# Seven products of block sums in place of eight for three quarters of an up projection, in a two-layer decoder step on one core

## The chip, the core and the metric

The kernel is one program on one core of a Trainium2 chip. Its time is the device time of one execution in microseconds (us). TensorE (PE) does the matmuls; VectorE (DVE), ScalarE (ACT) and GpSimd (POOL) do everything else; SyncE (SP) only issues transfers.

## The reference

Two layers of a decoder work on 576 tokens: one prompt of 512, and 8 samples of 8 new tokens. Each layer mixes tokens in three branches and then runs an MLP. What matters here, for the tokens x of one layer:

```python
rq, rk, rv, rg, sq, sk, sv, mq, g_ret, g_swa, g_mem = split(x @ w_in)
# retention, sliding-window attention, attention into 256 memory tokens
merged = sigmoid(g_ret) * ret_b + sigmoid(g_swa) * swa_b + sigmoid(g_mem) * mem_b
x = layer_norm(ALPHA * x + merged @ w_out, ln1_g, ln1_b)
h = jnp.square(jax.nn.relu(x @ w_up))             # (576, 1024) @ (1024, 4096)
return layer_norm(ALPHA * x + h @ w_down, ln2_g, ln2_b)   # (576, 4096) @ (4096, 1024)
```

The prompt attends to 256 memory tokens that the layer computes; each sample attends to memory keys and values of its own, which come from caches (`in_mck`, `in_mcv`).

## The kernel before

Activations are kept with features on the 128 partitions and tokens along the columns, in two token groups: A has 256 columns, B 320 (`NG`, `OFF`). All weights are laid out beforehand as 154 units per layer, each a tile of 128 x 8 x 128 f32 (512 KB), in the order in which they are used (`unit_order`); SP fetches them in that order from `in_wall`. An output tile of 128 features for one group is the sum of 8 slots of a unit over 1,024 inputs.

Matmuls run in fp32r. To keep the accuracy of f32, each operand is split into a rounded part and the rest, and each slot takes three matmuls: hi by xh, lo by xh, hi by xl (`gemm`). So one unit is 24 matmuls for group A (`pg<-A,...`) and 24 for B (`mstep`, `both`).

`split` prepares a unit. For `up` and `dn` units, ACT casts the raw tile to hi (CAST 128x1024), writes the negative of hi to lo (ACTIVATE 128x1024), and POOL issues a transfer that adds the raw tile to lo (accumulate DMA, `A<-A` or `B<-A` on POOL). So lo is there when that transfer has landed. The other units get lo by a subtraction on DVE or POOL. Tiles come from two pools of 25 (tag A) and 15 (tag B) buffers; a tile that finds none free waits for the last reader of the oldest.

The MLP stage goes through four chunks of the 4,096 hidden features: 8 `up` units, then 8 `dn` units. An `up` output is evacuated by ACT as relu, square, cast (`up_ev`), and a subtraction for its low part; a `dn` output is added by DVE onto `y` in SBUF.

The order of instructions on every engine is fixed while the program is built. `run` walks over the products; after every six matmuls `Filler.advance` emits other work that is due by a model of the engines (`Clock`), and `tick` emits the next unit's split when its use, as planned by `plan` with `mm_us` per matmul, is within `LOOK`, when no more than `cap` units are split and unused, and when ACT is free or the use is nearer than `LEAD` = 4 us. An engine then executes its rows strictly in that order. The program's instructions are all recorded by one helper (L331 before, L358 after), so that the names of tiles tell them apart.

In the sample part of the memory attention (`mem_sample`), scores `pa` of four samples are taken one after the other, 8 short matmuls each; two key tiles are loaded ahead by POOL, the others in turn as earlier samples' matmuls are emitted. The value tiles follow in the same way.

Of the kernel before, what the change touches and what calls it, by code (L numbers as in the profile page):

```python
# [21 lines left out]
NB = 8  # L22
# [4 lines left out]
NG = {"A": 256, "B": 320}  # L27
OFF = {"A": 0, "B": 256}
TOK = SEQ + NB * NT
UNITS = 154  # L30
SKEW_WO = 8
# [11 lines left out]
N_A = 25  # L43
N_B = 15
# [18 lines left out]
def unit_order():  # L63
    o = [("mk", m) for m in range(4)] + [("mv", i) for i in range(4)]
    for p in range(4):
        o += [("rk", p), ("rq", p), ("rv", p, 0), ("rv", p, 1), ("rg", 2 * p), ("rg", 2 * p + 1)]
    o += [("sv", 0), ("sk", 0)] + [("sq", m) for m in range(4)]
    for m in range(8):
        o += [("gr", m), ("br", m)]
    o += [("mq", m) for m in range(4)]  # L70
    for g, b in (("gs", "bs"), ("gm", "bm")):
        for i in range(4):
            o += [(g, 2 * i), (g, 2 * i + 1), (b, i)]
    o += [("wo", m) for m in range(8)]
    for c in range(4):
        o += [("up", c, m) for m in range(8)] + [("dn", c, m) for m in range(8)]
    return o


def pack_weights(w_in, w_br_ret, w_br_swa, w_br_mem, w_out, w_mem_kv, w_up, w_down):  # L80
# [13 lines left out]
    for l in range(DEPTH):  # L94
        wb_swa = w_br_swa[l][swa_rows]
        for u, key in enumerate(order):
# [29 lines left out]
            elif k == "up":  # L126
                v = full(w_up[l], (m * 8 + key[2]) * P + np.arange(P))
            else:
                v = full(w_down[l][m * 1024:(m + 1) * 1024], key[2] * P + np.arange(P))
# [4 lines left out]
def make_consts():  # L134
# [4 lines left out]
    pos = np.concatenate([np.arange(SEQ), np.tile(PAST + np.arange(NT), NB)]).astype(np.float32)  # L139
# [59 lines left out]
def mm_us(n):  # L199
    return n / 2400.0 + 0.0025  # L200


def plan():
    a, b = 24 * mm_us(256), 24 * mm_us(320)
    t, out = 0.0, []
    order = unit_order()
    for l in range(DEPTH):
        i = 0
        while i < UNITS:
            k = order[i][0]  # L210
            if k in ("mk", "mv"):
                out.append(t)
                t += a
            elif l and order[i] == ("rk", 0):
                out += [t, t + a]
                t += 2 * (a + b)
                i += 1
            elif k == "rv":
                out += [t, t]
                t += 4.67 * a  # L220
                i += 1
            elif order[i] in (("wo", 8 - SKEW_WO), ("up", 0, 0), ("dn", 3, 8 - dn_skew(l))):
                s = {"dn": dn_skew(l), "wo": SKEW_WO, "up": SKEW_UP}[k]
                for j in range(s):
                    out.append(t)
                    t += a if k != "dn" or l < DEPTH - 1 else b
                t += s * (b if k != "dn" or l < DEPTH - 1 else a)
                i += s - 1
            else:
                out.append(t)  # L230
                t += a + b
            i += 1
# [117 lines left out]
class Filler:  # L350
# [48 lines left out]

    def finish(self, gen):  # L400
# [15 lines left out]
class Builder:  # L416
    def __init__(self, nc, tc, I, O, coff, pools):
# [9 lines left out]
        self.done = -1  # L427
        self.cap = 4
        self.use = plan()
# [3 lines left out]
    def tile(self, shape, dt=F32, tag="A", bufs=None):  # L433
        self.n += 1
        bufs = bufs or {"A": N_A, "B": N_B}[tag]
# [16 lines left out]
    def u(self, n=320):  # L452
        return self.tile([P, 320], tag="u", bufs=5)[:, :n]

    def tt(self):
        return self.tile([P, 320], tag="t", bufs=4)
# [52 lines left out]
    def fetch(self, u):  # L509
        self.raw[u] = self.tile([P, 8, P], tag="A")  # L510
# [4 lines left out]
    def split(self, u):  # L515
        raw = self.raw.pop(u)
        k = unit_order()[u % UNITS]
        if k[0] == "wo":
            b = True
        elif k[0] in ("up", "dn"):  # L520
            b = u % 2 == 0
        else:
            b = k[0] in ("gr", "br") and u % 4 == 0
        tl = "B" if b else "A"
        hi = self.tile([P, 8, P], F32R)
        lo = self.tile([P, 8, P], F32R, tag=tl)
        if k[0] in ("up", "dn"):
# [5 lines left out]
        self.w[u] = (hi, lo)  # L533

    def tick(self):
        n, u = len(self.use), self.split_next
# [3 lines left out]
        urgent = self.use[u] < self.fill.t + LEAD  # L540
# [3 lines left out]
    def feed(self):  # L544
        while self.dma_next <= min(self.split_next + 2, len(self.use) - 1):
# [5 lines left out]
    def run(self, steps, cap=3):  # L551
# [5 lines left out]
        for i, (units, fn, tick) in enumerate(steps):  # L557
# [3 lines left out]
            for u in units:  # L561
                if last[u] == i:
                    self.done = max(self.done, u)
# [4 lines left out]
    def gemm(self, ps, u, slots, xs):  # L568
# [4 lines left out]
        for i, s in enumerate(slots):  # L573
            xh, xl = xs(i)
            mm(ps, lhsT=hi[:, s, :], rhs=xh, start=(i == 0), stop=False)
            mm(ps, lhsT=lo[:, s, :], rhs=xh, start=False, stop=False)
            mm(ps, lhsT=hi[:, s, :], rhs=xl, start=False, stop=(i == n - 1))
# [14 lines left out]

    def pair_tiles(self, dt=F32):
        return {"A": self.tile([P, 4, 256], dt, tag="A"), "B": self.tile([P, 4, 320], dt, tag="B")}

    def feat_tiles(self, nt):
        r = {}
        for g in "AB":
            r[g] = {"h": [], "l": []}
            for k in "hl":  # L600
                for j in range(nt):
                    r[g][k].append(self.tile([P, 4, NG[g]], F32R, tag=g))
        return r

    def load_x(self, X):
# [5 lines left out]
        def part(g, j):  # L611
            raw = self.tile([P, 4, NG[g]], tag=g)
# [9 lines left out]
        def split():  # L622
            for i in range(4):
# [5 lines left out]
                h = self.tile([P, 4, NG[g]], F32R, tag=g)  # L629
                lo = self.tile([P, 4, NG[g]], F32R, tag=g)  # L630
# [70 lines left out]
    def norm_ev(self, g, y, l, gi, eps, out, scale=None, bias=1.0):  # L701
# [33 lines left out]
        def half():  # L735
            c = st.pop("c")
            V.tensor_tensor(y[0], y[0], c.unsqueeze(1).to_broadcast([P, 4, n]), ALU.subtract)
            sq = self.tile([P, 4, n], tag=g)
# [7 lines left out]
        def last():  # L746
# [4 lines left out]
            t = self.tile([P, 320], tag="ln", bufs=2)[:, :n]  # L751
# [8 lines left out]
            r0 = self.tile([P, 320], tag="ln", bufs=2)[:, :n]  # L760
# [7 lines left out]
            a = self.tile([P, 320], tag="ln", bufs=2)[:, :n]  # L768
# [27 lines left out]
            if out is not None:  # L796
                out[g]["h"] += [self.tile([P, 4, n], F32R, tag=g) for _ in range(2)]
                out[g]["l"] += [self.tile([P, 4, n], F32R, tag=g) for _ in range(2)]
# [64 lines left out]

    def rope_evac(self, ps, out, o, n):
# [7 lines left out]
    def retention(self, l, p, qk, rv, sg, GR):  # L872
# [11 lines left out]
        yield Pe((qk, rv))  # L884
        v2 = self.tile([P, 2, 256], F32R)
        self.split_into(v2[:64, 0], v2[:64, 1], rv[:64, 4, :])
# [9 lines left out]
        for e in range(2):  # L896
            r = slice(e * 64, e * 64 + 64)
            for c in range(4):
                cs = slice(c * P, (c + 1) * P)
                T.matmul(pq[e][:, cs], lhsT=k[r, cs], rhs=q[r, cs], start=True, stop=True)  # L900
# [8 lines left out]
        for c in range(4):  # L909
            cs = slice(c * P, (c + 1) * P)  # L910
            T.transpose(pk[:, cs], k[:, cs], ident)
        px = [self.bank("a"), self.bank("a")]
        for e in range(2):
            r = slice(e * 64, e * 64 + 64)
            T.matmul(px[e][:64, P:P + 64], lhsT=k[r, 512:576], rhs=q[r, 512:576], start=True, stop=True)
        T.transpose(px[0][:64, 0:P], k[:, 512:576], ident)
# [17 lines left out]
        V.tensor_tensor(kq[:, 1].rearrange("p (c i) -> p c i", c=4), q[:, 0:512].rearrange("p (c i) -> p c i", c=4),  # L934
# [8 lines left out]
        for f in range(2):  # L943
            for e in range(2):
                r = slice(e * 64, e * 64 + 64)
                dst = self.qz[f * 64:f * 64 + 64, e, f * 32:f * 32 + 288].rearrange("p (b c) -> p b c", b=4)[:, :, 0:8]
                V.tensor_tensor(dst, q[r, 512 + f * 32:544 + f * 32].rearrange("p (b t) -> p b t", b=4),
# [11 lines left out]
        for bb in range(5):  # L959
            for e in range(2):  # L960
# [4 lines left out]
                else:  # L965
                    T.matmul(o, lhsT=ks[:, 256 + e * 64:320 + e * 64], rhs=rv[:64, 4, e * P:(e + 1) * P],
# [34 lines left out]
        gs = self.tile([P, P], tag="u", bufs=5)  # L1001
# [11 lines left out]
        wt = self.tile([P, 2, 512])  # L1013
        ws = self.tile([P, 2, 64], tag="ws", bufs=1)
# [8 lines left out]
        for e in range(2):  # L1023
            yield (ps[e],)
            V.scalar_tensor_tensor(wt[:, e], ps[e], gg[:, e:e + 1], sg[:, e, 0:512], ALU.mult, ALU.mult)
            V.scalar_tensor_tensor(ws[:, e], pt[:, e * 64:e * 64 + 64], gg[:, e:e + 1], sg[:, e, 512:576],
                                   ALU.mult, ALU.mult)
        yield (wt, ws)
        for src, g_, a, b in ((wt[:, :, 0:256], "A", 0, 256), (wt[:, :, 256:512], "B", 0, 256), (ws, "B", 256, 320)):
# [748 lines left out]
```

## Time and profile before

| | |
|---|---|
| time, median of 3 runs | 2186.92 us (2186.02 to 2187.66) |
| profiled execution | 2185.91 us, span 2184.1 us |
| granted TensorE clock, mean | 0.997 of full speed |
| busy in the span | PE 2147.9 us (98%), DVE 1060.2 (49%), ACT 846.9 (39%), POOL 411.2 (19%) |
| DMA | 130 GB/s mean |

The span runs from the first to the last instruction of the profiled execution; 1.8 us of that execution's time lie outside it. PE works in nearly all of it, so what bounds the kernel is looked for in PE's rows and its waits.

### The profile page before, as it was taken

Reading aid. Unit: us, or ns where it says so; the run is one execution under the profiler, and the core shown is the slowest. Engines: PE = TensorE matmul, PEld = TensorE weight load, DVE = VectorE, ACT = ScalarE, POOL = GpSimd, SP = SyncE. Lnnn points to the kernel's source line nnn. Section 1 sums busy time; section 2 is a strip of 40 time slices with the busy share of each in tenths; the row PEclk is TensorE's granted clock in tenths of the full one; section 3 lists DMA queues with packets and bytes.
Section 4 is the critical chain, followed back from the end, with each engine's and each line's share of the span. In section 5 each row is a group of like instructions: output and inputs, shape, how many; then the busy total and the mean of one; then the engine's idle time right before and its main releaser. Section 6 shows DMA issues by size and latency. Waiting matters only on the chain. (4 is left out here: it accounts for less than half of the span.)

```text
span 2184.1 us, 39229 instructions
## 1 busy us (share of the span) xinstructions
PE 2147.9 (98%) x16466; PEld 2089.6 (96%) x16466; DVE 1060.2 (49%) x2164; ACT 846.9 (39%) x1581; POOL 411.2 (19%) x400
## 2 busy tenths in 40 slices
PE   9999999999999999999999999999999999999996
PEld 9999999999999999999989998999999999999996
DVE  6666765455566111111876668554555751111127
ACT  3222234232146454636342221442221573636362
POOL 0222300011033111111432223000210321111113
PEclk9999999999999999999999999999999999999999
DMA  8222212334255867676452222123443557676661
GB/s 308 78 90 86 91 49 69 116 135 137 98 169 126 201 143 185 153 195 161 125 178 84 84 84 83 59 68 107 145 153 124 144 126 195 148 187 159 174 150 45
DMA packets 85168, 284.56 MB, mean 130 GB/s; under 512 B 9280, under 2 KB 19008, under 8 KB 84928
## 3 DMA queue, kind: packets, MB, share of 16 engines
q1 hardware_dynamic: 50944, 168.27, 22.2%
q0 software_dynamic: 28960, 105.92, 22.0%
q10 hardware_dynamic: 5088, 7.87, 1.1%
q8 instruction: 129, 2.11, 0.4%
q14 instruction: 47, 0.39, 0.1%
HBM read 200.89 MB, written 15.99 MB: 99 GB/s over the span
## 5 line engine op out<-in xcount | busy, mean ns | idle before, releaser
L331 PE MATMUL pg<-B,A 128*128 128x320 f32 x5920 | 1024.7, 310 | 2.4 <-DVE A L331 1.4
L331 PE MATMUL pg<-A,A 128*128 128x256 f32 (+1 forms) x6720 | 961.1, 286 | 12.1 <-DVE A L331 5.5
L331 PEld LDWEIGHTS pg<-A,A 128*128 128x128 f32 x6720 | 891.2, 192 | 28.9 <-issue 12.8
L331 PEld LDWEIGHTS pg<-B,A 128*128 128x128 f32 x5920 | 903.9, 188 | 7.5 <-issue 3.4
L331 ACT CAST A<-A 128x1024 fp32r<-128x1024 f32 (+4 forms) x316 | 294.0, 943 | 208.1 <-DVE A L331 73.1
L331 PE MATMUL pg<-A,B 128*128 128x256 f32 x1088 | 248.0, 283 | 0.0
L331 PE MATMUL pg<-B,B 128*128 128x320 f32 x704 | 217.5, 309 | 0.0
L331 DVE TENSOR_TENSOR A<-A,A 128x1024 fp32r<-128x1024 f32 (+3 forms) x173 | 191.1, 1115 | 49.6 <-ACT A L331 46.2
L331 PEld LDWEIGHTS pg<-A,B 128*128 128x128 f32 x1088 | 181.8, 192 | 0.0
L331 ACT ACTIVATE t<-pg 128x256 f32<-128x256 f32 (+1 forms) x128 | 52.5, 410 | 290.7 <-PE pg L331 290.5
L331 POOL TENSOR_TENSOR A<-A,A 128x1024 fp32r<-128x1024 f32 (+2 forms) x40 | 84.5, 2117 | 331.7 <-ACT A L331 273.6
L331 PEld LDWEIGHTS pg<-B,B 128*128 128x128 f32 x704 | 132.4, 188 | 0.0
L331 DVE TENSOR_TENSOR B<-u,B 128x320 fp32r<-128x320 f32 x80 | 39.4, 492 | 190.0 <-ACT B L331 190.0
L331 POOL DMA_DIRECT2D A<-A x64 | 55.7, 870 | 354.5 <-ACT u L331 177.1
L331 ACT ACTIVATE u<-pg 128x320 f32<-128x320 f32 (+1 forms) x128 | 51.4, 401 | 162.3 <-PE pg L331 162.1
L331 POOL DMA_DIRECT2D B<-A x64 | 55.0, 860 | 260.2 <-ACT B L331 115.8
L331 DVE TENSOR_TENSOR A<-u,A 128x256 fp32r<-128x256 f32 x72 | 30.5, 423 | 136.8 <-ACT A L331 129.0
L331 ACT ACTIVATE A<-A 128x1024 fp32r<-128x1024 f32 (+1 forms) x70 | 73.9, 1055 | 52.6 <-DMA B<-A 34.9
L331 DVE TENSOR_TENSOR B<-B,pg 128x320 f32<-128x320 f32 x56 | 27.0, 485 | 117.2 <-PE pg L331 117.1
L331 DVE TENSOR_TENSOR B<-B,u 128x256 f32<-128x256 f32 (+3 forms) x84 | 75.6, 908 | 2.4
L331 POOL TENSOR_TENSOR A<-A,cst 128x512 fp32r<-128x512 f32 x32 | 43.7, 1391 | 152.4 <-ACT A L331 152.4
L331 ACT ACTIVATE B<-A 128x1024 fp32r<-128x1024 f32 x64 | 67.4, 1053 | 0.0
(203 smaller groups left out, 1722.4 us busy)
## 6 DMA issues: line engine op xcount, KB each, us to landing
A<-in_wall SPq DMA_DIRECT2D x305, 512.0 KB, 3.5
B<-A POOLq DMA_DIRECT2D x64, 512.0 KB, 5.2
A<-A POOLq DMA_DIRECT2D x64, 512.0 KB, 5.3
A<-in_mck POOLq DMA_DIRECT2D x16, 512.0 KB, 4.2
A<-in_mcv POOLq DMA_DIRECT2D x16, 512.0 KB, 6.3
A<-in_s POOLq DMA_DIRECT2D x8, 512.0 KB, 4.1
out_state_s<-A POOLq DMA_DIRECT2D x8, 512.0 KB, 3.2
d<-A POOLq DMA_DIRECT2D x6, 512.0 KB, 7.7
```

The lines of the kernel that those rows point to most:

```text
L331: r = f(*a, **kw)
```

## The change

The token groups become equal: 288 columns each, tokens reordered so that each group has 32 sample tokens and 256 prompt tokens. The first 1,024 hidden features stay as 8 plain `up` units. The other 3,072 are computed in pairs of units (`ua`, `ub`): with the inputs cut into halves, the outputs into two and the tokens into two groups, the eight half products of a pair (2 outputs x 2 groups x 2 halves) are got from seven products of block sums (`pair_steps`, 12 matmuls of 288 columns each). The block sums of the weights are made by DVE (`block`), those of the activations once per layer (`sums`), and four of the seven results are combined by DVE subtractions from PSUM. The down units for the first 3,072 rows become `dh` units (two outputs of 128 by 512 rows), two of them behind each pair; the last 1,024 rows stay as 8 `dn` units. The two pools become one of 38 tiles, `tick` counts split tiles in use (`live`), and the plan's time per matmul goes from n/2400 + 0.0025 to n/2400 + 0.0134.

```diff
-NG = {"A": 256, "B": 320}
+NG = {"A": 288, "B": 288}
...
-    for c in range(4):
-        o += [("up", c, m) for m in range(8)] + [("dn", c, m) for m in range(8)]
+    o += [("up", m) for m in range(8)] + [("dh", 0, j) for j in ORDER_DH]
+    for q in range(2, 8):
+        for j in range(2):
+            o += [("ua", q, j), ("ub", q, j)]
+            if q < 7:
+                o += [("dh", q - 1, k) for k in ORDER_DH[2 * j:2 * j + 2]]
+    o += [("dn", m) for m in range(8)]
...
-    return n / 2400.0 + 0.0025
+    return n / 2400.0 + 0.0134
...
-        if k[0] in ("up", "dn"):
+        if k[1] in ("up", "dn", "dh"):
             self.nc.scalar.copy(hi, raw)
             self.nc.scalar.activation(lo, raw, AF.Copy, scale=-1.0)
             self.nc.gpsimd.dma_start(lo, raw, accum_op=ALU.add)
...
+    def block(self, u, b):
...
+        if b == 1:
+            sa, sb = self.tile([P, 8, P]), self.tile([P, 4, P], tag=("s", "rc")[u // 2 % 2], bufs=1)
...
+            V.tensor_tensor(sa.rearrange("p (e s) c -> p e s c", e=2), ra.rearrange("p (e s) c -> p e s c", e=2),
+                            rb[:, 0:4].unsqueeze(1).to_broadcast([P, 2, 4, P]), ALU.add)
+            V.tensor_tensor(sb, sa[:, 4:8], ra[:, 0:4], ALU.add)
...
+        w = self.tile([P, 8, P], F32R)
+        self.nc.scalar.copy(w[:, 0:4], src)
+        V.tensor_tensor(w[:, 4:8], src, w[:, 0:4].bitcast(F32), ALU.subtract)
...
-        if u >= n or u - self.done > self.cap or self.use[u] > self.fill.t + LOOK:
+        if i >= n or self.use[i] > self.fill.t + LOOK:
+            return
+        if sum(self.live.values()) + (2 if self.items[i][2] is None else 1) > 2 * self.cap:
             return
...
+    def pair_steps(self, key, XT, evac):
...
+        def e0():
+            st["s1"] = self.u()
+            S.copy(st["s1"], st["z"])
+
+        def e1():
+            sub("w", st.pop("v"), st.pop("s1"))
...
+        def e6():
+            sub("o", st.pop("y"), st.pop("w"))
+            evac(0, "B", st.pop("o"))
...
+    def sums(self, y, T):
...
+            V.tensor_tensor(r[0][:, 2:4], b22, b12, ALU.subtract)
+            V.tensor_tensor(r[0][:, 0:2], b11, b12, ALU.subtract)
+            V.tensor_tensor(r[1][:, 0:2], r[0][:, 2:4], b11, ALU.add)
+            V.tensor_tensor(r[1][:, 2:4], r[1][:, 0:2], b21, ALU.subtract)
...
+        for q in range(2, 8):
+            H.append(self.feat_tiles(1))
+            steps = []
+            for j in range(2):
+                def pev(i, g, ps, j=j, q=q):
+                    up_ev(2 * j + i, H[-1])(g, ps)
+                steps += self.pair_steps((l, "ua", q, j), XT, pev)
+                if q < 7:
+                    for k in ORDER_DH[2 * j:2 * j + 2]:
+                        steps += dh(q - 1, k, H[0])
+            self.run(steps, 3.5)
```

By the two programs, the fp32r matmuls into the projections' PSUM tiles go from 14,573 (7,925 of 256 columns and 6,648 of 320) to 14,285 (1,280 of 256 and 13,005 of 288). On ACT, casts of 1,024 elements go from 254 to 191, activations of 1,024 from 134 to 80, casts of 512 from 38 to 186; POOL's accumulate transfers go from 128 to 80.

Three places in the order of instructions carry the argument. The first is ACT before, in the second chunk's `up` units of layer 0: A1163 and A1164 are hi and lo of one unit; u1158, u1160 and u1165 are outputs under evacuation (relu from PSUM tile `pg`, square, cast).

```order
L331 ACTIVATE u1158_8488<-pg1154_8456 128x256
L331 ACTIVATE u1158_8488<-u1158_8488 128x256
L331 CAST A1146_8448<-u1158_8488 128x256
L331 ACTIVATE u1160_8518<-pg1159_8492 128x320
L331 ACTIVATE u1160_8518<-u1160_8518 128x320
L331 CAST B1150_8452<-u1160_8518 128x320
L331 CAST A1163_8538<-A1142_8402 128x1024
L331 ACTIVATE A1164_8539<-A1142_8402 128x1024
L331 ACTIVATE u1165_8555<-pg1161_8522 128x256
```

The split of A1164 stands behind the evacuation of pg1159; on PE, 192 matmuls lie between the last of pg1159 and the first of pg1189, the first tile that A1163 and A1164 are used for. The same place after the change is ACT in a pair of layer 0: pg1153 is one of the pair's PSUM tiles, u1167 and u1168 hold the combined outputs of its sixth and seventh product, T1172 and T1173 are hi and lo of the second `dh` unit behind the pair.

```order
L358 ACTIVATE u1166_8354<-pg1153_8265 128x288
L358 ACTIVATE u1166_8354<-u1166_8354 128x288
L358 CAST T1149_8261<-u1166_8354 128x288
L358 ACTIVATE u1167_8371<-u1167_8371 128x288 x2
L358 CAST T1149_8261<-u1167_8371 128x288
L358 ACTIVATE u1168_8389<-u1168_8389 128x288 x2
L358 CAST T1151_8263<-u1168_8389 128x288
L358 CAST T1172_8419<-T1133_8128 128x1024
L358 ACTIVATE T1173_8420<-T1133_8128 128x1024
```

Now the second `dh` unit is split behind the evacuation of the pair's seventh product. PE there, after the change, has the end of that product (pa1164), the first `dh` unit (hi T1160, lo T1161; 48 matmuls into pg1169, pg1170, pg1174 and pg1181, most left out) and then the second:

```order
L358 MATMUL pa1164_8324<-T1067_7527,T1157_8291 128x288
L358 MATMUL pg1169_8394<-T1039_7392,T1160_8304 128x288 [waits Activation_49]
L358 MATMUL pg1169_8394<-T1039_7392,T1161_8305 128x288 [waits DMASW7_49]
...
L358 MATMUL pg1181_8459<-T1042_7395,T1160_8304 128x288
L358 MATMUL pg1182_8473<-T1039_7392,T1172_8419 128x288 [waits DVE_49,Activation_49]
L358 MATMUL pg1182_8473<-T1039_7392,T1173_8420 128x288 [waits DMASW0_49]
L358 MATMUL pg1182_8473<-T1040_7393,T1172_8419 128x288
```

So 49 matmuls lie between the seventh product and the first one that reads T1173, and that one waits for the transfer (DMASW0). The third place is PE in the sample part of the memory attention after the change: T690, T691, T724 and T725 are the keys of four samples.

```order
L358 MATMUL pa721_5175<-T690_4972,T720_5170 32x256 [waits DMASW3_49,DVE_49]
L358 MATMUL pa721_5175<-T690_4972,T720_5170 32x256 x3
L358 MATMUL pa721_5175<-T691_4974,T720_5170 32x256 [waits DMASW4_49,DVE_49]
L358 MATMUL pa721_5175<-T691_4974,T720_5170 32x256 x3
L358 MATMUL pa721_5175<-T724_5207,T720_5170 32x256 [waits DMASW5_49,DVE_49]
L358 MATMUL pa721_5175<-T724_5207,T720_5170 32x256 x3
L358 MATMUL pa721_5175<-T725_5213,T720_5170 32x256 [waits DMASW6_49,DVE_49]
L358 MATMUL pa721_5175<-T725_5213,T720_5170 32x256 x3
```

The rows read the same before the change; what moved is on POOL. The load of T725 now has to wait until PE has read T690, since all 38 tiles are taken and T690's place is the next to come free; the load of its counterpart before (A720) found another place and waited for none of these matmuls.

## Rows read from the trace of the kernel before

**Rows 1.** The page: busy time and instructions of each engine.
```profile
PE 2147.9 (98%) x16466; PEld 2089.6 (96%) x16466; DVE 1060.2 (49%) x2164; ACT 846.9 (39%) x1581; POOL 411.2 (19%) x400
```
**Rows 2.** PE's waits: releaser, us in total, times, longest.
```profile
PE pg L331 <- DVE A L331: 6.9, 4, 4.4
PE pg L331 <- DVE B L331: 5.2, 5, 1.8
...
PE pa L331 <- DMA A<-in_mck: 1.3, 2, 1.0
```
**Rows 3.** Windows in both MLP stages: length, busy PE, PEld, DVE, ACT, POOL, PEclk, DMA.
```profile
640.00:1030.00 390.00, 389.48 (x2903) 389.21 (x2902) 92.65 (x175) 210.90 (x343) 68.34 (x80) 1.00 0.68 165
1790.00:2100.00 310.00, 310.00 (x2316) 310.00 (x2316) 44.46 (x97) 155.53 (x243) 43.04 (x51) 1.00 0.70 171
```
**Rows 4.** Timeline of PE, from 499.8 and from 450.2 us: start, duration, instruction.
```profile
499.90 1.93 PE L331 MATMUL pg<-B,A 128*128 128x320 f32 x12
501.66 1.60 PE L331 MATMUL pg<-A,A 128*128 128x256 f32 x12
503.10 0.46 PE L331 MATMUL pg<-B,A 128*128 128x320 f32 x2
...
450.48 0.39 PE L331 MATMUL pa<-A,A 128*128 128x512 f32 x1
450.71 0.40 PE L331 MATMUL pa<-A,B 128*128 128x512 f32 x1
```
**Rows 5.** Timeline of ACT and POOL in a chunk's `up` units, from 792 us.
```profile
792.85 0.44 ACT L331 ACTIVATE u<-pg 128x320 f32<-128x320 f32 x1 [1.91 <-PE pg L331]
...
794.19 1.04 ACT L331 CAST A<-A 128x1024 fp32r<-128x1024 f32 x1
795.14 1.05 ACT L331 ACTIVATE A<-A 128x1024 fp32r<-128x1024 f32 x1
...
796.49 0.86 POOL L331 DMA_DIRECT2D A<-A  x1 [5.54 <-ACT u L331]
```
**Rows 6.** Timeline: an accumulate transfer, and the ACT instruction that waits for it.
```profile
862.54 0.86 POOL L331 DMA_DIRECT2D A<-A  x1 [6.05 <-ACT A L331]
...
867.23 1.05 ACT L331 CAST A<-A 128x1024 fp32r<-128x1024 f32 x1 [4.99 <-DMA A<-A]
```
**Rows 7.** POOL's transfers into A tiles, 783 to 820 us, then 640 to 1050.
```profile
DMA to landing us min/median/max: 4.5/4.6/4.7
...
DMA to landing us min/median/max: 4.5/5.1/11.0
```
**Rows 8.** The page: DMA issues, engine, count, KB each, median us to landing.
```profile
A<-A POOLq DMA_DIRECT2D x64, 512.0 KB, 5.3
A<-in_mck POOLq DMA_DIRECT2D x16, 512.0 KB, 4.2
A<-in_mcv POOLq DMA_DIRECT2D x16, 512.0 KB, 6.3
```
**Rows 9.** The page: DVE groups, busy time, mean ns of one, idle before.
```profile
L331 DVE TENSOR_TENSOR B<-u,B 128x320 fp32r<-128x320 f32 x80 | 39.4, 492 | 190.0 <-ACT B L331 190.0
...
L331 DVE TENSOR_TENSOR A<-u,A 128x256 fp32r<-128x256 f32 x72 | 30.5, 423 | 136.8 <-ACT A L331 129.0
```
**Rows 10.** Timeline of PE in the memory attention, sample part of layer 0.
```profile
474.84 1.50 PE L331 MATMUL pa<-A,B 128*32 128x256 f32 x24
477.30 0.64 PE L331 MATMUL pa<-A,B 128*32 128x256 f32 x8 [0.96 <-DMA A<-in_mck]
```
**Rows 11.** Timeline of PE: two waits, at 1107.8 and at 271.6 us.
```profile
1112.23 1.44 PE L331 MATMUL pg<-A,A 128*128 128x256 f32 x5 [4.42 <-DVE A L331]
...
273.46 0.71 PE L331 MATMUL pg<-A,A 128*128 128x256 f32 x4 [1.84 <-DVE B L331]
```
**Rows 12.** Windows around these waits, columns as in rows 3.
```profile
270.00:276.00 6.00, 4.16 (x33) 3.92 (x32) 5.93 (x14) 0.00 (x0) 1.09 (x1) 1.00 0.04 16
...
1111.80:1115.10 3.30, 2.87 (x14) 2.87 (x14) 3.23 (x7) 1.25 (x3) 0.34 (x1) 0.50 0.00 0
```

More of the change, by code (lines that the diff above doesn't have):

```diff
@@ L398, in step, with idle, push @@
             self.gens.remove(rec)
+    def idle(self, gen):
+        return all(rec[0] is not gen for rec in self.gens)
+    def push(self, gen):
+        self.step(next(rec for rec in self.gens if rec[0] is gen))
     def finish(self, gen):
@@ L513, in fetch, with split @@
             next(self.between, lambda: None)()
-    def split(self, u):
-        raw = self.raw.pop(u)
[L517 to L524, printed above, removed]
+    def split(self, i):
+        u, k, b = self.items[i]
+        if b is not None:
+            self.w[i] = self.block(u, b)
+            self.live[i] = 1
+            return
+        raw = self.raw.pop(u)
         hi = self.tile([P, 8, P], F32R)
-        lo = self.tile([P, 8, P], F32R, tag=tl)
-        if k[0] in ("up", "dn"):
+        lo = self.tile([P, 8, P], F32R)
+        if k[1] in ("up", "dn", "dh"):
             self.nc.scalar.copy(hi, raw)
@@ L796, in last @@
             if out is not None:
-                out[g]["h"] += [self.tile([P, 4, n], F32R, tag=g) for _ in range(2)]
-                out[g]["l"] += [self.tile([P, 4, n], F32R, tag=g) for _ in range(2)]
+                out[g]["h"] += [self.tile([P, 4, n], F32R) for _ in range(2)]
+                out[g]["l"] += [self.tile([P, 4, n], F32R) for _ in range(2)]
             z = [mult(i) for i in range(4)]
@@ L1289, in mem_sample @@
         den = self.small(1, "zd")
-        p = self.tile([P, 256], tag="u", bufs=5)
+        p = self.u(256)
         yield (ps,)
@@ L1552, in mem_parts @@
                 nc.scalar.dma_start(t, src)
-                parts += [self.tile(src.shape, F32R, tag=k) for k in ("AB" if src is mvd else "BB")]
+                parts += [self.tile(src.shape, F32R) for _ in range(2)]
                 yield (t,)
@@ L1604, in load_y @@
             for g in "AB":
-                y[g] = [self.tile([P, 4, NG[g]], tag=g) for _ in range(2)]
+                y[g] = [self.tile([P, 4, NG[g]]) for _ in range(2)]
                 for j in range(2):
@@ L1673, in e, with dh, ev @@
+        H = [self.feat_tiles(1), self.feat_tiles(1)]
+        steps = []
+        for m, g in [(m, g) for g in "AB" for m in range(SKEW_UP)] \
+                + [(m, g) for m in range(SKEW_UP, 8) for g in "AB"]:
+            steps.append(self.lazy(self.mstep(uid["up", m], g, X1, up_ev(m, H[m // 4])), lambda g=g: n1[g].st["last"]))
+        self.run(steps, SKEW_UP)
+        self.fill.drain()
+        Ts = []
+        tg = self.sums(y, Ts)
+        def dh(q, k, src):
+            def ev(m):
                 def e(g, ps):
-                    yt = y[g][m // 4][:, m % 4, :]
@@ L1675, in e @@
-                    if c == 0:
+                    if q == 0:
+                        while len(Ts) <= (m % 4) // 2 and not self.fill.idle(tg):
+                            self.fill.push(tg)
+                        yt = y[g][m // 4][:, m % 4, :]
                         V.scalar_tensor_tensor(yt, yt, ALPHA, ps, ALU.mult, ALU.add)
                     else:
+                        yt = y[g][m // 4][:, m % 4, :]
                         V.tensor_tensor(yt, yt, ps, ALU.add)
                 return e
-            keys = [("dn", c, m) for m in range(8)]
@@ L1681, in layer @@
-            if c < 3:
-                steps = []
-                for m in range(8):
-                    steps += self.both(uid[keys[m]], H, ev(m))
-                self.run(steps, 5)
-                continue
+            r = []
+            for e in range(2):
+                r += self.both(uid["dh", q, k], src, ev(2 * k + e), range(4 * e, 4 * e + 4))
+            return r
+        self.fill.add(tg, 2)
+        steps = []
+        for k in ORDER_DH:
+            steps += dh(0, k, H[0])
+        self.run(steps, 3)
@@ L1687, in layer @@
+        del Ts, XT, X1
+        H = {g: {k: [h[g][k][0] for h in H] for k in "hl"} for g in "AB"}
+        if True:
+            keys = [("dn", m) for m in range(8)]
             n2 = {g: self.norm_ev(g, y[g], l, 16, EPS, X2, bias=0.0 if g == "A" and X2 is None else 1.0) for g in "AB"}
```

395 lines of the change are left out of this document (242 added, 153 removed).

## The prediction

> **What bounds the kernel now.** I read the page's busy times first: PE is at work for 2147.9 of 2184.1 us and every other engine for less than half of the span [rows 1]. The windows of the MLP stages are fuller still: 389.48 of 390 us and 310.00 of 310 [rows 3]. So in the stages that the change rewrites, matmul time is all there is, and other engines matter only where PE comes to wait for them. The table of PE's waits says how little it waits now: the largest sums are 6.9 and 5.2 us [rows 2]. There is nothing to win from waits; a gain must come out of matmul time, and each new wait counts in full.
>
> The reader should then take one matmul's interval from the timeline: 12 of 320 columns start at 499.90, 12 of 256 at 501.66, the next at 503.10, so 146.7 and 120.0 ns each; two of 512 are 0.23 us apart [rows 4]. All three lie on n/2.4 + 13.4 ns (120.1, 146.7, 226.7). A matmul of 288 is then 133.4 ns.
>
> **Matmuls removed.** Before, 7,925 x 120.0 + 6,648 x 146.7 ns = 1,926.3 us. After, 1,280 x 120.0 + 13,005 x 133.4 = 1,888.5 us. Equal groups alone change nothing (120.0 + 146.7 = 2 x 133.4); the gain is 288 matmuls of 288 columns: **-38.4 us**. One product in eight is saved on only three quarters of one of many projections, so the saving is 2% of the matmuls. Bounds for a matmul of 288 are the neighbours' 120.0 and 146.7; I take the line, which holds at three widths.
>
> **The second down unit behind each pair.** This is the largest term. Between two pairs stand two `dh` units, and ACT splits the second behind the evacuation of the pair's seventh product, while before the split stood 192 matmuls, about 25 us, ahead of its use. Now the chain, from the end of the seventh product's last matmul:
> - DVE's subtraction, 288 columns from PSUM: 256 take 423 ns and 320 take 492 [rows 9], so 0.46, and 0.04 to reach it.
> - relu, square and cast on ACT: 792.85 to 794.19 is 1.34 us at 320 columns [rows 5]; at 288 about 1.3, with 0.04 ahead.
> - the cast to hi and the negative copy to lo: 794.19 to 795.14 is 0.95, then 1.05 to the copy's end; POOL's transfer starts at 796.49, 0.3 later [rows 5].
> - the transfer: issued at 862.54, its reader starts at 867.23, 4.7 us [rows 6]; the medians are 4.6 in one stretch and 5.1 in another [rows 7] and 5.3 over the kernel [rows 8]. I take 4.7, since SP then fetches little.
>
> This is 0.04 + 0.46 + 0.04 + 1.3 + 0.95 + 1.05 + 0.3 + 4.7 = 8.84, and 0.16 more because a matmul ends after its successor has started: 9.0 us. PE covers it with 49 matmuls: 49 x 133.4 ns = 6.5 us. PE waits 2.5 us, in 5 quarters x 2 pairs x 2 layers = 20 places: **+50** (46 with a landing of 4.5, 60 with 5.2). The first `dh` unit is split one evacuation or more earlier and has the same 6.4 us of cover again; I leave it at nothing, with a wait of a few tenths if the landing is slow.
>
> **Other units split late.** The eighth `up` unit's split stands behind the evacuation of the product two before it, with 25 matmuls (3.3 us) as cover: 0.04 + 1.3 + 2.0 + 0.3 + 4.7 = 8.4, so 5.1 in each layer, **+10** (9 to 12). The first `dn` unit, straight behind the last pair, is split behind the evacuation of the sixth product, when ACT is still draining the fourth and fifth; ACT gets to it about when the seventh product ends, so that 0.2 + 2.0 + 0.3 + 4.7 = 7.2 us of PE's time lie open in each layer: **+14.5** (13 to 18).
>
> **Block sums.** Weight sums, subtractions and casts add work to DVE and ACT, but a pair with two `dh` units is 180 matmuls, 24 us, and by durations as in [rows 5, 9] they put some 14 us on DVE and 12.5 on ACT in it; PE hides this. The activations' sums are another matter: DVE makes them at the start of the first `dh` quarter, where PE has three PSUM banks to run ahead. By 1.08 ns per column more [rows 9], a sum of 576 columns is 0.77 us and the low part of 1,152 is 1.4; a half is four and two of these, 5.9 us, of which some 2.3 lie beside two banks of matmuls (24 x 133.4 ns less the pending evacuation): **+7** for two layers, between nothing and 14. In the last quarter no `dh` unit lies between the two pairs; I put 2 us in each layer, **+4** (0 to 8).
>
> **The sample part of the memory attention.** Three key tiles' matmuls take 1.50 us and PE now waits 0.96 for the fourth [rows 10]. With the loading of the fourth tile moved behind the first tile's matmuls, PE has the second and third as cover, about 0.84 + 0.1 us, against a load of 4.2 (keys) or 6.3 (values) [rows 8] and a few tenths to start it. I take 4 us each for keys and values, in the first half of both layers: 16, less the 1.3 that PE waits for keys now [rows 2]: **+14.7** (11 to 22). POOL holds no other row that PE needs in that time.
>
> **Clock.** After a wait of 4.42 us PE's granted clock was 0.50, the 1.2 GHz level, for 3.3 us, which costs half of that, 1.65; after a wait of 1.84 it stayed at 1.00 [rows 11, 12]. For the four longest waits of above: **+6.6** (0 to 13, with the memory loads). The norm behind the last matmul has 288 columns where it had 256: **+1.5** (0 to 3).
>
> **Sum.** -38.4 + 50 + 10.2 + 14.5 + 7 + 4 + 14.7 + 6.6 + 1.5 = +70. On the span of 2184.1 that is 2254; the execution lies 1.8 outside it, 2256, and the median of the three runs is 1.0 above the profiled one: **2257 us**. The terms' lower bounds give -38.4 + 46 + 9 + 13 + 0 + 0 + 11 + 0 + 0 = +41, 2228; the upper ones -38.4 + 60 + 12 + 18 + 14 + 8 + 20.7 + 13 + 3 = +110, 2297.
>
> **Rivals.**
> 1. *The accumulate lands sooner than any row.* Behind the seventh product PE stands and little else is being fetched. Each microsecond less takes 24 off the sum (20 + 2 + 2 places): at 1.5 us less, -36, 2221. Against it: the least of all those transfers in both stretches is 4.5 [rows 7]. The Trainium skill ("DMA: Bandwidth & Descriptors", section on the anatomy of one DMA on the SWDGE path) fits a transfer issued by GpSimd as 2.0 us plus its bytes over 436 GB/s. For 512 KB that would be an estimate of 3.2 us; the rows disagree with it for the accumulating kind. Splits that come a little earlier than I count give the same time. Chance 0.12.
> 2. *It lands later.* The DMA share is already 0.68 to 0.70 in the MLP [rows 3], and the maximum there is 11.0 [rows 7]. At the 6.3 of the slowest kind of load [rows 8], +38, 2295. For it: 5.1 to 5.3 as medians; against it: 4.6 in the regular stretch. Chance 0.13.
> 3. *Waits of 2.5 us drop the clock as well.* The rows show 1.84 without and 4.42 with; at 1.65 each, 20 places are +33, 2290. Chance 0.08.
> 4. *The other sign: a matmul of 288 costs less than the line.* No row has this width. At the interval of 256, 13,005 x 13.4 ns are another 174 us less: 2083. It decides from 70,000 / 13,005 = 5.4 ns below the line, 128 ns. Against it is that 512 columns too lie on the line. Chance 0.04.
> 5. *The seven products save nothing on PE*, because the smaller accumulations cost what they save: 38 more, 2295. The same three matmuls per slot in the same order speak against it. Chance 0.01.
>
> The forecast has the other 0.62, within 2228 to 2285.
>
> **How the numbers follow.** The three runs before lie within 0.04% of their median, so 0.2% (4.4 us) about marks what can be told from no change. The range takes in the forecast's bounds and rivals 1 to 3: 2215 to 2300. Rival 4 holds nearly all of the chance of faster, 0.05 with one for several small errors together; 0.02 for no change; 0.93 for slower.
>
> **What would show it.** PE's waits in the profile of after should have a group of about 20 for a transfer into T by POOL, some 2.5 us each, at the second matmul of a `dh` unit, and two longer ones each at the eighth `up` and the first `dn` unit; the MLP windows should show PE at about 90%, and matmuls of 288 columns 133.4 ns apart. Waits for in_mck and in_mcv should hold about 16 us. If the waits for transfers sum to under 30 us, my chain is wrong, most likely where ACT's place in it is taken from the order; if they are there and the time is not, the interval is.

## The result: 2308 us, 5.5% slower

The changed kernel takes 2308.28 us (median of 4 runs, 2301.58 to 2311.97), the kernel before 2187.29 us (2186.02 to 2188.34): ratio 1.055, 95% interval 1.0523 to 1.0577. The prediction was 2257 us in a range to 2300. Its direction and its waits were right; one term, TensorE's clock, was far too small. The profiled execution took 2310.27 us with a span of 2308.0, 123.9 us longer than that of before.

The page of the kernel after, busy times and transfers (these answer to [rows 1, 8]):

```profile
PE 2167.4 (94%) x16180; PEld 2096.4 (91%) x16180; DVE 1346.4 (58%) x2660; ACT 859.2 (37%) x1682; POOL 354.9 (15%) x345
...
T<-T POOLq DMA_DIRECT2D x80, 512.0 KB, 5.3
T<-in_mck POOLq DMA_DIRECT2D x16, 512.0 KB, 4.3
T<-in_mcv POOLq DMA_DIRECT2D x16, 512.0 KB, 6.3
```

286 instructions fewer on PE, and yet PE is busy 19.5 us longer. If the matmuls had only become fewer, its busy time would have fallen by 38.4 us. So 58 us of PE's busy time have come on top of the matmuls' own, apart from the waits in the table below.

PE's waits after (they answer to [rows 2]): releaser, us in total, times, longest.

```profile
PE pg L358 <- DMA T<-T: 70.8, 26, 7.7
PE pg L358 <- DVE T L358: 18.5, 12, 4.8
PE pa L358 <- DMA T<-in_mcv: 13.3, 4, 5.2
PE pa L358 <- DMA T<-in_mck: 9.8, 5, 2.8
PE pg L358 <- ACT T L358: 6.0, 4, 2.0
```

All groups of this table sum to 125.8 us (the largest five are shown), those of before to 22.5: 103 us more. -38.4 of matmuls, +103 of waits and these 58 make +123, the difference of the spans within 1 us; since the 58 is what is left over of the busy time, this sum closes by itself and doesn't say what the 58 are.

The chain behind a pair's seventh product, as the prediction added it up, is seen in the timeline of all engines (start, duration, instruction):

```profile
788.64 6.69 PE L358 MATMUL pg<-T,T 128*128 128x288 f32 x49
...
788.83 0.46 DVE L358 TENSOR_TENSOR u<-pa,u 128x288 f32<-128x288 f32 x1 [0.78 <-PE pa L358]
...
789.33 0.92 ACT L358 ACTIVATE u<-u 128x288 f32<-128x288 f32 x2 [0.22 <-DVE u L358]
790.28 0.43 ACT L358 CAST T<-u 128x288 fp32r<-128x288 f32 x1
...
790.62 1.05 ACT L358 CAST T<-T 128x1024 fp32r<-128x1024 f32 x1
...
791.58 1.05 ACT L358 ACTIVATE T<-T 128x1024 fp32r<-128x1024 f32 x1
...
792.92 0.86 POOL L358 DMA_DIRECT2D T<-T  x1 [9.30 <-ACT T L358]
...
797.49 1.84 PE L358 MATMUL pg<-T,T 128*128 128x288 f32 x11 [2.16 <-DMA T<-T]
```

The 48 matmuls of the first `dh` unit and the first one of the second start at 788.64, while the seventh product's last matmul is still ending; DVE, ACT and POOL follow one behind the other, the transfer takes 4.57 us, and PE goes on at 797.49: 8.85 us for what was counted at 9.0. The transfer agrees with [rows 6, 7]. By the fit of the Trainium skill ("DMA: Bandwidth & Descriptors", section on the anatomy of one DMA on the SWDGE path) an estimate for 512 KB is 3.2 us; the measured 4.57 us disagrees with it.

What the prediction did not count enough is seen in PE's timeline and in windows there (length, busy PE, PEld, DVE, ACT, POOL, granted clock, DMA share, GB/s):

```profile
785.44 3.36 PE L358 MATMUL pa<-T,T 128*128 128x288 f32 x24
788.64 6.69 PE L358 MATMUL pg<-T,T 128*128 128x288 f32 x49
797.49 11.23 PE L358 MATMUL pg<-T,T 128*128 128x288 f32 x71 [2.16 <-DMA T<-T]
...
825.45 11.25 PE L358 MATMUL pg<-T,T 128*128 128x288 f32 x71 [2.20 <-DMA T<-T]
...
882.32 9.73 PE L358 MATMUL pg<-T,T 128*128 128x288 f32 x71 [3.15 <-DMA T<-T]
```

```profile
799.00:802.20 3.20, 3.20 (x15) 3.20 (x14) 1.66 (x3) 0.62 (x1) 0.00 (x0) 0.50 0.00 0
802.60:820.00 17.40, 17.40 (x132) 17.40 (x132) 7.25 (x17) 9.36 (x18) 0.86 (x1) 1.00 0.52 152
882.40:892.00 9.60, 9.60 (x72) 9.60 (x73) 4.85 (x9) 2.56 (x5) 0.00 (x0) 1.00 0.16 56
```

At full clock 24 matmuls take 788.64 - 785.44 = 3.20 us, 133.3 ns each: the line held for 288 columns (it answers to [rows 4]). After the wait of 2.16 us the same 71 matmuls last 11.23 us in place of 9.73: PE has resumed, and a moment later the granted clock is 0.50, the 1.2 GHz level, for some 3.4 us, though PE is busy throughout. After [rows 11, 12] I had taken waits of this length as harmless. They are not always followed by it (the wait of 3.15 us ending at 882.32 was not). Of the pairs' 20 places, 18 have a wait of 2.1 to 3.2 us, and 13 of these are followed by it.

The mean granted clock says how long it is in all: 0.971 over 2308.0 us where it was 0.997. With only two levels, 2 x 0.029 x 2308 = 134 us ran at the lower one, and 14 us before. Not all of this costs time, since part of it lies in PE's waits and behind its last matmul. The sum of the windows at the lower level in the trace of after (in all, busy PE, PEld, DVE, ACT, POOL):

```profile
sum 133.49, PE 103.70 PEld 102.06 DVE 56.87 ACT 33.98 POOL 8.48; mean PE 3.84 PEld 3.78 DVE 2.11 ACT 1.26 POOL 0.31
```

Before, PE is busy in 2.95 of the 14 us. So about 101 us more of PE's work ran at the lower level, and at 1.50 us lost in 3.4, as above, about 45 us of the 58 are the clock (an estimate). Another 7 us are the ends of matmuls: 24 in a row last 3.36 us by their row and 3.20 to the next one's start, so each wait costs 0.16 us more than its row says, and there are 43 more of them. What the last 6 us are is not shown.

### The profile page after: what moved, and what is told of

The parts are those of the page before. It is cut to its first block, busy times and chain, and to the rows that moved or that the text cites. A ratio compares the mean times of both kernels' runs of the same rounds, so it can differ in the third digit from the quotient of the medians.

```text
span 2308.0 us, 39149 instructions
## 1 busy us (share of the span) xinstructions
PE 2167.4 (94%) x16180; PEld 2096.4 (91%) x16180; DVE 1346.4 (58%) x2660; ACT 859.2 (37%) x1682; POOL 354.9 (15%) x345
## 5 line engine op out<-in xcount | busy, mean ns | idle before, releaser
L358 PE MATMUL pg<-T,T 128*128 128x288 f32 (+1 forms) x12992 | 1822.5, 300 | 95.4 <-DMA T<-T 70.8
L358 PEld LDWEIGHTS pg<-T,T 128*128 128x128 f32 x12992 | 1777.6, 193 | 125.3 <-DMA T<-T 77.2
L358 DVE TENSOR_TENSOR T<-T,T 128x1024 fp32r<-128x1024 f32 (+7 forms) x433 | 414.3, 970 | 106.2 <-ACT T L358 100.0
L358 ACT CAST T<-T 128x1024 fp32r<-128x1024 f32 (+7 forms) x461 | 344.9, 776 | 298.6 <-DVE T L358 247.5
L358 PE MATMUL pa<-T,T 128*128 128x288 f32 (+9 forms) x2216 | 285.4, 310 | 24.5 <-DMA T<-in_mcv 13.3
L358 PEld LDWEIGHTS pa<-T,T 128*128 128x128 f32 (+3 forms) x2216 | 240.8, 169 | 49.4 <-issue 21.4
L358 POOL TENSOR_TENSOR T<-T,T 128x1024 fp32r<-128x1024 f32 (+2 forms) x50 | 102.2, 2055 | 675.4 <-ACT T L358 423.6
L358 DVE TENSOR_TENSOR T<-T,pg 128x288 f32<-128x288 f32 x208 | 93.8, 452 | 171.7 <-PE pg L358 171.3
L358 ACT ACTIVATE u<-u 128x288 f32<-128x288 f32 x200 | 89.2, 446 | 70.8 <-DVE u L358 66.7
L358 DVE TENSOR_TENSOR T<-T,u 128x288 f32<-128x288 f32 (+2 forms) x132 | 106.5, 817 | 3.7
L358 ACT ACTIVATE T<-T 128x1024 fp32r<-128x1024 f32 (+1 forms) x92 | 98.4, 1070 | 15.9 <-DVE T L358 15.9
```

The lines of the kernel that those rows point to most:

```text
L358: r = f(*a, **kw)
```

## The experiments

Medians and ratios to the kernel before, which ran beside them at medians of 2187.3 to 2190.1 us. Clock is the mean granted clock of the profiled execution.

| run | what | median us | ratio, 95% interval | clock |
|---|---|---|---|---|
| after | the change | 2308.3 | 1.055, 1.0523 to 1.0577 | 0.971 |
| e1_fill | after, 18 unused matmuls in each of the pairs' 20 waits | 2286.0 | 1.0443, 1.0426 to 1.0460 | 0.982 |
| e8_fill9 | after, 9 unused matmuls | 2288.3 | 1.0443, 1.0424 to 1.0461 | 0.976 |
| e2_sub | after, subtraction for the transfer | 2260.3 | 1.0322, 1.0305 to 1.0339 | 0.983 |
| e4_mem | after, tiles freed for memory loads | 2278.3 | 1.0406, 1.0383 to 1.0428 | 0.972 |
| e5_early | after, MLP units split earlier | 2222.0 | 1.0143, 1.0128 to 1.0158 | 0.984 |
| e6_both | e5 and e4 together, and the first unit of a pair urgent within 6 us | 2194.5 | 1.0018, 1.0009 to 1.0028 | 0.989 |
| e3_groups | equal groups, no products | 2242.2 | 1.0239, 1.0224 to 1.0255 | 0.983 |
| e7_groups2 | e3 with both corrections | 2202.0 | 1.0055, 1.0040 to 1.0070 | 0.992 |
| e10_nopool | e6, some low parts off POOL | 2178.8 | 0.9954, 0.9939 to 0.9969 | 0.992 |
| e9_dn | e10, low parts of the first three `dn` units by DVE, `dn` urgency as in after | 2162.5 | 0.9879, 0.9863 to 0.9896 | 0.995 |

**Do the waits lower the clock, or does the work?** The two theories part when PE has something to do in the wait.

```diff
+        x = X1["A"]["h"][0]
+
+        def fill():
+            ps = self.bank("a")[:, :288]
+            for _ in range(18):
+                nc.tensor.matmul(ps, lhsT=x[:, 0, 0:P], rhs=x[:, 1, :], start=True, stop=True)
...
-                    for k in ORDER_DH[2 * j:2 * j + 2]:
+                    for n, k in enumerate(ORDER_DH[2 * j:2 * j + 2]):
+                        if n:
+                            steps.append(([], fill, 0.0))
                         steps += dh(q - 1, k, H[0])
```

> 18 more matmuls of 288 columns (2.4 us) stand on PE between the first and the second down unit behind each pair, where PE waits; their result is not used and nothing else changes. Theory 1 (the waits themselves cost a stretch at the lower clock): the half-rate stretches behind these 20 waits, some 51 us long together in the profile of after, go away, which gives back about 25 us, less 3 us because 2.4 us is a little more than the usual wait: 2283 to 2290 us, mean granted clock 0.98 or more. Theory 2 (the pairs' work mix or load lowers the clock, not the waits): more matmul work, so 2308 us or more and a clock of 0.971 or less.

2286.0 us, where theory 1 stood, and PE's clock is at its lower level for 82 us in all in place of 134. In the MLP windows of the run, the columns as above:

```profile
720.00:1000.00 280.00, 276.76 (x2064) 275.34 (x2063) 143.50 (x269) 139.19 (x249) 19.15 (x23) 1.00 0.45 119
1860.00:2140.00 280.00, 275.69 (x2056) 274.02 (x2055) 145.66 (x275) 140.74 (x250) 19.95 (x24) 1.00 0.45 120
```

The same windows of the kernel after have

```profile
720.00:1000.00 280.00, 259.08 (x1834) 256.49 (x1833) 138.83 (x259) 133.34 (x237) 18.30 (x22) 0.95 0.42 111
1860.00:2140.00 280.00, 255.83 (x1811) 252.93 (x1810) 136.36 (x258) 134.93 (x241) 19.11 (x23) 0.95 0.43 112
```

More work on the same engine made the kernel 22 us faster, because work that is of no use held the clock at 1.00. So the waits cause the slow stretches, not the load of the products. With half the filling:

> As the first run, with 9 unused matmuls (1.2 us) instead of 18 between the two down units, so that waits of about 1 us stay in the 20 places. Theory 1, with short waits harmless: the clock stays at its higher level there as with 18, and the time is that of the first run, 2280 to 2290 us. Rival (each wait that long lowers it too): 2295 to 2308 us.

2288.3 us. In 16 of the 20 places this run waits 0.9 to 1.4 us and keeps the clock; in four the wait is longer, and all four are followed by the lower clock. The two kinds stand side by side in PE's timeline:

```profile
798.83 9.73 PE L358 MATMUL pg<-T,T 128*128 128x288 f32 x71 [0.96 <-DMA T<-T]
...
825.95 9.72 PE L358 MATMUL pg<-T,T 128*128 128x288 f32 x71 [1.31 <-DMA T<-T]
...
880.94 11.23 PE L358 MATMUL pg<-T,T 128*128 128x288 f32 x71 [3.13 <-DMA T<-T]
...
936.18 11.24 PE L358 MATMUL pg<-T,T 128*128 128x288 f32 x71 [1.92 <-DMA T<-T]
```

Waits of 0.96 and 1.31 us cost themselves alone, those of 3.13 and 1.92 another 1.5 us each. The other two of the four are 1.91 and 1.92 us long, hardly more than the 1.84 that passed without a drop in [rows 11, 12].

**Where do the waits come from?** First the transfer was taken out of the chain: hi by ACT, lo by a subtraction (`dh` on POOL, `up` and `dn` on DVE or POOL).

```diff
-        if k[1] in ("up", "dn", "dh"):
-            self.nc.scalar.copy(hi, raw)
-            self.nc.scalar.activation(lo, raw, AF.Copy, scale=-1.0)
-            self.nc.gpsimd.dma_start(lo, raw, accum_op=ALU.add)
+        if k[1] == "dh":
+            self.nc.scalar.copy(hi, raw)
+            self.nc.gpsimd.tensor_tensor(lo, raw, hi.bitcast(F32), ALU.subtract)
```

> The low part of up, dn and dh units is got by a subtraction (dh on POOL, up and dn on DVE or POOL) instead of the negative copy and the accumulate transfer. Theory 1: the chain behind the seventh product is 1.84 + 0.95 + some 2.4 = 5.3 us, less than its 6.5 us of cover, so that the 20 waits go, and those of the eighth up and first dn unit fall to about 0.4 and 2.5 us: 65 us less waiting, and some 38 us of lower clock less with it, about 2205 us (2195 to 2220). Theory 2 (the clock doesn't hang on these waits): 65 us less only, about 2243 us.

2260.3 us: a miss by 55 for theory 1, and beyond theory 2 as well. The waits for transfers are gone, as expected; a new one has come. Timeline of POOL, DVE and PE in a pair:

```profile
791.55 2.40 POOL L358 TENSOR_TENSOR T<-T,T 128x1024 fp32r<-128x1024 f32 x1 [7.70 <-ACT T L358]
...
792.22 2.28 DVE L358 TENSOR_TENSOR T<-T,T 128x512 fp32r<-128x512 f32 x1
...
798.21 8.26 PE L358 MATMUL pg<-T,T 128*128 128x288 f32 x60 [1.61 <-DVE T L358]
```

A DVE subtraction of 512 columns, 0.69 us elsewhere in the run, lasts 2.28 and ends half a microsecond behind POOL's. DVE's evacuations come late, and PE waits 1.6 us in place of 2.2, 68.4 us for DVE in all. The run thus says that the transfer was what PE waited for, and not what its removal is worth. None of these 20 waits of 1.61 to 1.68 us is followed by the lower clock. All of PE's waits together are only some 22 us shorter than in after, while the run is 48 us faster: PE's busy time fell too, from 2167.4 to 2139.4 us, with the clock at 0.983.

Then only the time of the splits was changed. The planner emits a split when ACT is free by its model, or else when the use is within `LEAD`; behind a pair, by that model, ACT is not free in time.

```diff
-        urgent = self.use[i] < self.fill.t + LEAD
+        urgent = self.use[i] < self.fill.t + (16.0 if self.items[i][1][1] in ('dh', 'up', 'dn') else LEAD)
```

> Only the planner's urgency is changed: up, dn and dh units are split when their planned use is within 16 us instead of 4, as soon as the count of split tiles allows it. By the order, the second dh unit's split then stands ahead of the last evacuations of its pair, the eighth up unit's two products earlier; the first dn unit's does not move. Theory 1 (the splits come too late, and the waits lower the clock): waits for accumulate transfers fall from 71 to 12 to 18 us, some 0.5 us x 20 of waiting for DVE comes in their place, and about 30 us of lower clock go: 2220 to 2240 us. Rival (the transfers are slow in themselves, wherever they are issued): 2290 to 2308 us.

2222.0 us. The transfers are as long as before, but 86 us are gone by one number. PE's waits in this run:

```profile
PE pg L358 <- DVE T L358: 19.8, 15, 4.8
PE pg L358 <- DMA T<-T: 15.4, 3, 8.6
PE pa L358 <- DMA T<-in_mcv: 13.6, 5, 5.6
PE pa L358 <- DMA T<-in_mck: 9.0, 5, 2.4
```

Of 26 waits for accumulate transfers three are left, at the first `dn` units above all (8.6 us in layer 0), whose split still starts only 1.5 us ahead of its use. 55 us of waiting for these transfers went, and PE's busy time fell by 30 us with it, to 2137.7, at a clock of 0.984.

**The equal groups by themselves.** The MLP of the kernel before was put back on groups of 288, with the single pool.

> Only the equal groups of 288, the one pool of 38 tiles and the new planning constants; the MLP goes by four chunks of 8 up and 8 dn units as in the kernel before, with no products of block sums. Theory 1: matmul time as before (a matmul of 288 columns on the line between 256 and 320), plus the waits of after that are outside the pairs: about 22 us more for memory tiles, 11 at the eighth up unit, 3 at the layers' starts, and 10 to 18 us of lower clock behind these: 2230 to 2242 us. Rival: a matmul of 288 lies off the line, then the MLP windows show it and the time is off by 130 us per 10 ns. Rival: the memory waits come from the crowding by pairs; then about 2205 us.

2242.2 us, the upper end of theory 1. So 53 of the 121 us come without the products. PE's waits in this run hold the memory loads and, twice 5.4 us, the eighth `up` unit's transfer:

```profile
PE pa L346 <- DMA T<-in_mcv: 11.4, 3, 5.0
PE pg L346 <- DMA T<-T: 10.8, 2, 5.4
PE pa L346 <- DMA T<-in_mck: 8.3, 5, 2.6
```

These and the clock behind them are most of the 53 us. The memory waits were then taken from the changed kernel:

```diff
-        self.run(steps)
+        self.run(steps, 2)
```

> The changed kernel with at most two units split ahead, instead of three, while the branch units of the second branch run, so that tiles are free when POOL wants them for the sample part of the memory attention. Theory 1: the waits for in_mck and in_mcv fall from 23 to under 6 us, and about 10 us of lower clock go with them: 2278 to 2290 us. Rival (the loads are late by their own landing time, not for want of a tile): 2308 us, waits as before.

2278.3 us; waits for in_mcv fall from 13.3 to 3.4 us and those for in_mck leave the table. The two corrections together, and the first unit of each pair (`ua`) urgent within 6 us:

> As the run before (products' blocks urgent within 6 us too), and with at most two units split ahead in the branch stage, which frees tiles for the memory loads. Theory 1: the two effects add, 30 us less again: 2190 to 2210 us, which is at or a little above the kernel before. What is left of the distance to it minus 38 us should stand in PE's waits for DVE and in half-rate stretches.

2194.5 us: level with the kernel before, 0.2% above it. The same two for equal groups alone:

> Equal groups alone (no products of block sums), with the same two corrections: up and dn units urgent within 16 us, at most two units split ahead in the branch stage. Theory 1: of the 53 us that equal groups cost, the memory waits (17), the eighth up unit's (11) and the clock behind them (20) go: 2190 to 2200 us. Rival (a matmul of 288 columns is dearer than the line, or the single pool costs in other places): 2215 us or more.

2202.0 us, 2 us over the expected range and far from its rival. Between the last two runs stand the products themselves: they save 7.5 us, not 38. PE waits 17 us longer in e6 than in e7 (46 against 29 us in all), 13.5 of it for transfers, nearly all at the first `dn` units, and by the time that PE is busy at the lower clock (27.5 against 17.7 us) that is worth 4 to 5 us more. Some 8 us of the 38 show in neither; no run was made to find them.

**What is left.** In e6 PE waits 4.8 us in each layer's window-attention projections. There POOL runs five subtractions in a row; timeline of POOL and DVE:

```profile
259.48 10.80 POOL L358 TENSOR_TENSOR T<-T,T 128x1024 fp32r<-128x1024 f32 x5
...
260.63 9.98 DVE L358 TENSOR_TENSOR u<-u,rope 128x288 f32<-128x288 f32 x1
...
272.57 13.25 PE L358 MATMUL pg<-T,T 128*128 128x288 f32 x78 [4.81 <-DVE T L358]
```

```diff
-    def split_into(self, hi, lo, src, flexible=False):
+    def split_into(self, hi, lo, src, flexible=False, vector=False):
...
-        e = self.pick(hi) if flexible else self.nc.vector
+        e = self.pick(hi) if flexible and not vector else self.nc.vector
...
-            self.split_into(hi, lo, raw, True)
+            self.split_into(hi, lo, raw, True, k[1] in ("sv", "sk", "sq") or k[1] in ("gr", "br") and k[2] < 3)
```

> As the sixth run, with only the second of these two edits: nine low parts a layer on DVE instead of POOL, where POOL has five subtractions of 1,024 columns in a row and a DVE instruction of 288 columns lasted 10 us beside them. Theory (DVE stands still while POOL's subtraction runs, so that moving it to DVE frees more than it costs): no DVE instruction of 288 columns there is over 1 us, PE's waits of 4.8 us at 273 us and at the same place of the second layer go, and the half-rate stretches behind them: 2175 to 2185 us. Rival (DVE has too much to do there): waits for DVE stay or grow, 2190 to 2205 us.

2178.8 us, as the first theory had it: some 15 us less by giving DVE more to do, and the two waits of 4.8 us are gone. DVE and POOL at that place now:

```profile
261.06 0.45 DVE L358 TENSOR_TENSOR u<-u,rope 128x288 f32<-128x288 f32 x1
261.19 3.23 POOL L358 TENSOR_TENSOR T<-T,T 128x576 fp32r<-128x576 f32 x2 [1.28 <-ACT T L358]
261.54 1.58 DVE L358 TENSOR_TENSOR T<-T,u 128x288 f32<-128x288 f32 x1
263.05 2.46 DVE L358 TENSOR_TENSOR T<-T,T 128x1024 fp32r<-128x1024 f32 x1
```

The instruction that took 9.98 us takes 0.45. One of 288 columns still takes 1.58 beside POOL's shorter work, where none over 1 us was expected. Then the last late splits were taken from the transfers too (`if k[1] in ("up", "dh") or k[1] == "dn" and k[2] > 2` ahead of the accumulate, and the subtraction on DVE); in this run `dn` units are again urgent within 4 us only:

> As the sixth run (urgent splits, tiles freed), with the low parts of the first three dn units got by a subtraction on DVE instead of the accumulate transfer, and those of the units around the start of the gate stage (sv, sk, sq, the first three gr and br) on DVE instead of POOL. Theory 1: the last waits for accumulate transfers (13.5 us) fall to about 4 us of waiting for DVE, the waits of 4.8 us at each layer's sq units go, and 24 of the 37 us at half rate with them: 30 us less than the sixth run, 2155 to 2175 us, below the kernel before. Rival (DVE is the bound in these places): 2185 us or more, with longer waits for DVE.

2162.5 us, 1.2% faster than the kernel before, and as expected. PE's waits for transfers and for DVE, and its window over the MLP of the first layer:

```profile
PE pg L358 <- DVE T L358: 13.1, 15, 2.3
...
PE pg L358 <- DMA T<-T: 1.1, 2, 0.6
```

```profile
640.00:1010.00 370.00, 367.34 (x2723) 363.18 (x2721) 217.46 (x395) 205.50 (x375) 53.84 (x64) 1.00 0.48 126
```

PE is busy for 2121.6 us in this run, 26.3 less than before the change, at nearly the same clock (0.995 against 0.997). So most of the 38.4 us of matmul time does show once the waits are gone. What the products alone are worth in the end is not shown: no run has the edits of e10 and e9 without them, and e7, without the products, has the two waits of 4.8 us that e10 removes.

## Why the prediction was wrong, step by step

**Matmuls, -38.4.** The interval was right: 133.3 ns at 288 columns, where 133.4 was taken. (The prediction's two sums stand 37.8 apart, not 38.4; this is rounding.) That all of it becomes time is not borne out: some 8 us stay missing between e6 and e7.

**The second down unit, +50.** Right in mechanism and nearly in size. The chain took 8.85 us where 9.0 was counted. In 18 of the 20 places PE waits 2.1 to 3.2 us where 2.5 was said, in the other two twice 0.6 to 1.4 us, and all of them sum to 47 (70.8 less 2 x 5.4, 7.7 and 5.4). e5 shows that the place of the split in ACT's order is the cause: the same transfers, split earlier, are not waited for.

**The eighth up unit, +10, and the first dn unit, +14.5.** Right for the eighth up unit: 5.39 us at 718.01 and the same in layer 1, where 5.1 was counted. At the first dn unit PE waits 2.01 us for ACT's cast, does one matmul, and waits 7.66 for the transfer until 1089.12 (2.01 and 5.38 in layer 1): 17.1 in all, within the bounds of 13 to 18.

**Block sums, +7 and +4.** PE waits 1.4 and 0.3 us in each layer at the first `dh` quarter, 3.4 in all, and 0.33 for DVE between the pairs of the last quarter, where 2 were put: both within their bounds.

**Memory loads, +14.7.** 23.1 us less the 1.3 of before, 21.8: mis-sized, at the upper bound. In the first half of the samples the keys cost 8.6 us and the values 10.2, where 8 each were counted; the second half, which was left out, has another 4.3. The step itself holds: with tiles freed (e4) most of the waits go.

**Clock, +6.6 (0 to 13).** This is the step that failed. It priced "the four longest waits of above" and let the 20 waits of 2.5 us go free, on a single row of 1.84 us without a drop. Measured is about 45 us: 13 of the pairs' 18 waits of 2.1 to 3.2 us are followed by 3.4 us or more at 1.2 GHz, and the waits of about 5 us and more elsewhere by 6.8 us and more in most places, where I had 3.3 us from the one row of before. e1 shows that the waits cause it, 22 us in the pairs' places alone. So this one term makes some 38 of the miss of 51 us. The waits make another 10: they were counted at 100 us more than before and came out at 103 by their rows, 110 with the 0.16 us that each costs beyond its row.

**Rivals.** The third, that waits of 2.5 us drop the clock as well, is what happened in 13 of the 20 places, with a chance of 0.08. Its price of +33 was more than these places cost (22 us by e1), and its time of 2290 was still short, because it left four other waits at 1.65 us each and the rest at nothing. Rivals 1 and 2 (the transfer lands sooner or later) did not come about in the place shown: 4.57 us; in four of the 20 places the wait is 1 us longer. Rival 4 falls with the interval of 133.3 ns, rival 5 with e6 against e7.

What stays open is why a wait of 3.15 us passed without a drop while one of 2.16, and in e8 one of 1.92, did not; no run here was made to tell what decides.

## What to carry to other kernels

A new wait of the engine that bounds the kernel is priced twice: by its length, and by the slow stretch that may follow it, and where rows show one wait with and one without, the waits between them belong into the sum at a price near that of the bad case, not at nothing. A change that makes the evacuations a chain over several engines moves everything that is queued behind them; ask of each operand that a transfer completes how many matmuls now stand between its issue and its use. Here a saving of 2% of the matmuls made the kernel faster only with the splits moved ahead of their use and the memory tiles freed.

## What the runs showed of the hardware that was not expected

Unused matmuls made the kernel faster: 18 in each of 20 waits, 22 us less (e1). PE's idle time of about 1 us, at 0.96 and 1.31, was not followed by the lower clock, nor were the 20 waits of 1.61 to 1.68 us in e2's pairs; three of 1.91 to 1.92 us in e8 were, and 13 of 18 of 2.1 to 3.2 us in after. The length alone does not decide: a wait of 1.68 us at 1077.46 in e2 was followed by it, two of 3.1 us in after were not.

A DVE instruction on two SBUF operands stood still while POOL's subtractions ran: 288 columns took 9.98 us beside five of POOL's, where 0.45 us is usual (e6), and went back to 0.45 when POOL's were moved (e10); 512 columns took 2.28 in place of 0.69 (e2). An evacuation that read PSUM beside POOL's subtraction kept its 0.46 (at 791.84 in e2). The Trainium skill ("SBUF — State Buffer", section "SBUF: two separate sides") says that DVE, with two SBUF inputs, and a GpSimd instruction that reads SBUF share one pair of ports, that whichever starts first has it for its whole instruction, and that the other is blocked. The rows agree, and add that all five of POOL's instructions in a row (259.48 to 270.28 in e6) passed before DVE's ended at 270.61.
